# Other PSUM banks for the first projections of a hybrid decoder's mixer, and for what follows it

## The chip, the cores and the metric

The kernel runs on one core of one Trainium2 chip. The metric is the time of one execution on the device in microseconds, as the median of several runs. One execution was also taken by the hardware profiler; the views below come from it. The engines are TensorE (PE in the views; its weight loads, which overlap the matmuls, are PEld), VectorE (DVE), ScalarE (ACT), GpSimd (POOL) and SyncE (SP). TensorE writes to PSUM, 8 banks of 128 partitions by 512 fp32 values; VectorE and ScalarE read it from there.

## The reference

A decoder trunk of two layers, 512 tokens by 1024 channels, fp32. Each layer is

```python
x = x + 0.5 * swiglu(rms_norm(x, ffn1_norm[l]), ffn1_w_in[l], ffn1_w_out[l])
z = rms_norm(x, mix_norm[l]) @ mix_w_in[l]
z_fox, z_moba, z_rwkv = jnp.split(z, [FOX_IN, FOX_IN + MOBA_IN], axis=-1)
y = concatenate([fox_mixer(z_fox, ...), rwkv7_mixer(z_rwkv, ...), moba_mixer(z_moba, ...)])
x = x + y @ mix_w_out[l]
x = x + memory_cross_attention(rms_norm(x, xattn_norm[l]), rms_norm(mem, xattn_mem_norm[l]), ...)
x = x + 0.5 * swiglu(rms_norm(x, ffn2_norm[l]), ffn2_w_in[l], ffn2_w_out[l])
```

FoX is causal softmax attention with a forget gate (4 heads of 64), RWKV-7 a linear recurrence over the 512 tokens (8 heads of 64, done in blocks of 64 tokens, two heads at a time), MoBA a block-sparse causal attention (4 heads of 64). The cross-attention has 4 heads of 128 over 256 memory tokens.

## The kernel before

**Tiling.** x lies in SBUF transposed, 8 chunks of 128 channels by 512 tokens. All large matmuls are done in three passes: an operand is split into a high part (rounded to the matmul's fp32r) and a low rest, and `three` (lines 149 to 154) multiplies high by high, high by low and low by high into one PSUM bank. A projection of 128 columns (`zproj`) is 24 matmuls of 128x128 by 512 into one bank. Its weights are loaded by SyncE (`load_raw`, wraw, 3 buffers), and `split` (lines 137 to 147) makes whi on ScalarE and wlo on VectorE, two buffers each.

**Who empties a bank.** The norm's factor for each token is multiplied in when the bank is emptied on VectorE: `shift` (zt, line 523) for the projections of the recurrence, `heads_t` (p, line 499) for heads of the attentions. For this they need rsb, which comes from the norm's sum (`norm_sum`, line 247) and its spread over the partitions (`norm_spread`, line 256); the mixer issues the sum behind its first projection and the spread behind its second one.

**The mixer.** `ORDER` (line 37) is an order written out by hand: R, V and K with a number are the projections of the recurrence for one pair of heads, p stands for three more (p0 for decay and rate, p1 and p2 for the gates, p2 with the forget gates of FoX, 36 columns in all), fq, fk, fv, mq, mk, mv are the projections of the two attentions, s (scaled), g (gram), r (rows), i (inverse), t (transitions) and y (states) the six steps of the recurrence, and f with two digits a step of FoX's attention. A planner gives each engine its instructions in a fixed order before the run; it goes by priorities that fall along `ORDER`, with a lead for some kinds (`PRI`), and takes what it takes to be ready. So a unit that waits for a bank can be overtaken in the plan, but on the chip each engine's order is fixed.

**PSUM of the recurrence.** Eight banks in two pools, the first with ts twice and acc, the second with sp twice, tx, and ty twice: `RP` and `RPW`, lines 49 to 53. All first projections go to the one acc bank, but those that `ACC` (line 56) names: K0 to sp and p1 to tx. The ts banks belong to the transitions and the states, `TAGS`, and are first used by them after the first inverse. The scaled step, the norm's sum and spread and the forget gates use tx.

**PSUM of the mixer's end and the cross-attention.** `BP` and `BPW`: the first pool has acc twice and pt twice, the second po twice, the third sp twice. These pools lie over those of the recurrence, and a tile waits for the last reader of what lay in its bank. acc takes projections (of the memory and the queries) and the mixer's output projection, sp the scores, pt the transposed softmax, po the output of the attention and, under the name st, the norm's sum and spread. `ORDER2` has four kinds of work: steps of MoBA's attention (two digits), m (a piece of the memory's keys and values, `mem_kv`: transposes at line 1082, casts at 1086 and 1087, four key heads, two halves of the values), c (casts of the mixer's output) and w (its output projection). `ORDER3` is the cross-attention: sum, spread, z (a query projection), n (its norm), m, and attention steps.

Of the kernel before, what the change touches and what calls it, by code (L numbers as in the profile page):

```python
# [6 lines left out]
F32 = mybir.dt.float32  # L7
# [8 lines left out]
P = 128  # L16
# [24 lines left out]
ORDER2 = "31 11 10 m c0 01 21 00 c1 c2 m c4 x c5 c3 m c6 w3 m 20 m w6 m 30 w4 c7 w1 w5 w2 w0"  # L41

ORDER3 = "sum spread z1 z0 n1 z2 n0 m n2 02 z3 00 n3 12 03 10 13 01 11"
BP = {"acc": 2, "po": 2, "sp": 2, "pt": 2}

TAGS = {"s": "tx", "g": "ty", "r": "ty", "i": "ty", "t": "ts", "y": "ts"}

LATE = {"y2": 1, "G": 0, "Pf": 1, "KX": 1, "tk1": 0, "V2": 0, "gs0": 2, "gs1": 2, "ER": 1, "BN": 1, "KV": 2, "AR": 2, "tk2": 1, "g2": 1, "var": 2, "DC": 2, "p": 2, "a": 2, "zr": 0, "e": 0, "lw": 1, "zv": 1, "zk": 0}
RPW = {"ts": 0, "sp": 1, "acc": 0, "tx": 1, "ty": 1}
BPW = {"acc": 0, "sp": 2, "pt": 0, "po": 1}  # L50

RW = {"e": 2, "tk1": 2, "tk2": 2, "zr": 2, "zv": 2, "ER": 2, "zk": 2, "BN": 2}
RP = {"acc": 1, "tx": 1, "ty": 2, "ts": 2, "sp": 2}
WP = {"wraw": 3, "whi": 2, "wlo": 2}

ACC = {"K0": "sp", "p1": "tx"}
EARLY = 2

LINE = 512
# [39 lines left out]
def f32(ap):  # L99
    return ap.bitcast(F32)  # L100
# [15 lines left out]
class Trunk:  # L116
# [410 lines left out]
    def rwkv_prep(self, l, ap, rp, at, ab):  # L527
        nc, rw = self.nc, self.rw
        w = self.ins['mix_w_in'][l]
        self.tw = rw.tile([P, S], F32, name="tw", tag="tw")  # L530
        self.acc = ACC.get("p0", "acc")
        ps = self.zproj(ap, *self.weights(w[:, Z_LO:Z_LO + P]), P)
# [3 lines left out]
        for i, m in ((0, P), (1, 32)):  # L536
            g = rw.tile([P, S], F32, name=f"gs{i}", tag=f"gs{i}")
            self.acc = ACC.get(f"p{i + 1}", "acc")
            if i == 0:
# [469 lines left out]
    def softmax_pt(self, at, bp, sps, n):  # L1009

        nc = self.nc
        p = at.tile([P, 2, S], F32, name="p", tag="p")
        pT = at.tile([P, 2, S], F32, name="pT", tag="pT")
        mx = at.tile([P, 2], F32, name="mx", tag="mx")
        sm = at.tile([P, 2], F32, name="sm", tag="sm")
        for h in range(2):
            ph, m, s = p[:, h, :n], mx[:, h:h + 1], sm[:, h:h + 1]
            nc.vector.tensor_reduce(m, sps[h][:, :n], axis=AX.X, op=ALU.max, negate=True)
            nc.scalar.activation(ph, sps[h][:, :n], AF.Exp, bias=m, accum_out=s)
            nc.vector.reciprocal(s, s)  # L1020
            nc.vector.tensor_scalar(ph, ph, s, None, op0=ALU.mult)
            pt = bp.tile([P, 512], F32, name="pt", tag="pt" if "pt" in bp.bufs else "sp")
            for j in range(n // P):
                nc.tensor.transpose(pt[:, j * P:(j + 1) * P], ph[:, j * P:(j + 1) * P], self.ident)  # L1024
            self.cp(f"pT{h}", pT[:, h, :n], pt[:, :n])
        return pT.rearrange("p h (j q) -> p h j q", q=P)
# [86 lines left out]
    def xattn(self, l, xp, bp, mem):  # L1113
        nc = self.nc
        mm = nc.tensor.matmul
        oh = xp.tile([P, 4, S], F32R, name="oh", tag="oh")
        ol = xp.tile([P, 4, S], F32R, name="ol", tag="ol")
        w = self.ins['xattn_w_q'][l]
        fin = {}
        for o in self.order(ORDER3, PRI3, lambda o: "a" if o[0] in "01" else o[0]):  # L1120
            if o[0] == "z":
                h = int(o[1])
                q = xp.tile([P, S], F32, name=f"xqT{h}", tag=f"xqT{h}")
                fin[h] = q, self.heads_t(w[:, h * P:(h + 1) * P], bp, xp, bp, q, P, self.dpar[:, l, 13:14])
            elif o == "m":
                next(mem)
            elif o in ("sum", "spread"):
                getattr(self, "norm_" + o)(bp.tile([P, 512], F32, name="psx", tag="st"))
            elif o[0] == "n":
                fin[int(o[1])][1]()  # L1130
            else:
                u, t = int(o[0]), int(o[1])
                tq = slice(t * P, (t + 1) * P)
                sps = [bp.tile([P, 512], F32, name="sp", tag="sp") for _ in range(2)]
                for i in range(2):
                    mm(sps[i][:, :256], fin[2 * u + i][0][:, tq], self.mkT[:, 2 * u + i, :], start=True, stop=True)
                pT = self.softmax_pt(xp, bp, sps, 256)
                po = bp.tile([P, 512], F32, name="po", tag="po")
                for i in range(2):
                    h = 2 * u + i  # L1140
                    for j in range(2):
                        mm(po[:, i * P:(i + 1) * P], self.mv[:, j, h * P:(h + 1) * P], pT[:, i, j, :], start=j == 0, stop=j == 1)
                src = po[:, :256].rearrange("p (h q) -> p h q", h=2)
                o = oh[:, 2 * u:2 * u + 2, tq]
                nc.scalar.activation(o, src, AF.Copy)
                nc.vector.tensor_tensor(ol[:, 2 * u:2 * u + 2, tq], src, f32(o), op=ALU.subtract)
        return oh, ol

    def mixer_and_xattn(self, l):
        tc, nc = self.tc, self.nc  # L1150

        def sb(name, bufs=1):
            return tc.tile_pool(name=name, bufs=bufs, reuse_waits="tile")

        def pp(name, bufs=1):
            return tc.tile_pool(name=name, bufs=bufs, space=PSUM, reuse_waits="tile")
# [7 lines left out]
        with sb("raw") as raw:  # L1164
# [9 lines left out]
            with sb("rw") as rw0, sb("rwm") as rw1, sb("rwl") as rw2, pp("rp") as rp0, pp("rps") as rp1, pp("rpt") as rp2:  # L1174
# [55 lines left out]
                for o in self.order(ORDER, PRI, lambda o: "q" if o in parts and o != "p" else o[0]):  # L1230
                    self.acc = ACC.get(o, "acc")
                    if o in parts:
# [8 lines left out]
            with sb("kv") as kv, pp("bp") as bp0, pp("bps") as bp1, pp("bpt") as bp2:  # L1241
                bp = TagPool((bp0, bp1, bp2), BP, {"st": "po"}, BPW)
                mem = self.mem_kv(l, kv, bp)
# [120 lines left out]
```

## Time and profile before

| | us |
|---|---|
| median of 3 runs | 2577.13 (2576.03 to 2581.13) |
| profiled execution | 2587.6 |
| its span, first to last instruction | 2585.9 |
| TensorE busy | 2495.8 (97%) |
| VectorE, ScalarE, GpSimd busy | 1346.3, 864.3, 490.2 |
| mean granted clock of TensorE | 0.977 |

A line of a timeline reads: start, duration, engine, line, operation, output and inputs by the program's names, shape, count, and in brackets the idle time of the engine before it with what ended it. A line of the waits reads: who waited, for which instruction, total us, times, longest. In the table by stretches each engine has its busy time and its count; PEclk is the granted share of the full clock. Layer 0's mixer begins at 388, its recurrence ends at about 763, its cross-attention runs from 856 to 922; in layer 1 these are 1671, 2036, 2131 and 2195.

### The profile page before, as it was taken

The page shows a single profiled execution, that of the slowest core. Times are in us where ns is not written, and L with a number is a line of the kernel's source. Part 1 is how long each engine was busy: PE and PEld are TensorE (multiplying, and loading weights), DVE is VectorE, ACT ScalarE, POOL GpSimd, SP SyncE. Part 2 cuts the span into 40 slices and gives each one's busy share as a digit, 9 for nine tenths or more (in the row PEclk, how much of TensorE's full clock was granted, in tenths as well). Part 3 has the DMA queues.
Part 4 walks back from the last instruction along what each step waited for, and adds up shares of the span by engine and source line. Part 5 has one row for each costly group of instructions (what it writes and reads, how often), then busy time and mean ns, then how long its engine had stood idle before and what let it go on. Part 6 is the DMA issues. An engine that isn't in the chain of part 4 may idle for free.

```text
span 2585.9 us, 35209 instructions
## 1 busy us (share of the span) xinstructions
PE 2495.8 (97%) x13976; PEld 2030.0 (79%) x13976; DVE 1346.3 (52%) x2503; ACT 864.3 (33%) x1401; POOL 490.2 (19%) x613
## 2 busy tenths in 40 slices
PE   8999998999989899999999999998999899999999
PEld 6888886787768788888888888767877677888887
DVE  5434444666755664343444444455767666544444
ACT  4222232333343353232332222332334543422222
POOL 4212120222210122020221111202322110221211
PEclk9999999998979999999999999999989999999999
DMA  4333342221212223333333333422222121333332
GB/s 141 98 98 98 96 127 67 67 67 34 73 33 84 62 80 98 98 98 98 88 100 98 97 99 90 125 69 70 53 48 59 50 84 46 110 98 98 96 95 86
DMA packets 434880, 218.41 MB, mean 84 GB/s; under 512 B 63856, under 2 KB 428828, under 8 KB 434716
## 3 DMA queue, kind: packets, MB, share of 16 engines
q1 hardware_dynamic: 431948, 212.36, 29.0%
q10 hardware_dynamic: 2448, 2.76, 0.3%
q8 instruction: 110, 1.80, 0.3%
q0 software_dynamic: 320, 1.05, 0.1%
q14 instruction: 54, 0.44, 0.1%
HBM read 205.64 MB, written 10.49 MB: 84 GB/s over the span
## 4 chain that ended last, share of the span: by engine, by line
PE 86%; DVE 5%; POOL 2%; ACT 2%; DMA 2%; issue 1%; SPq 1%; ACTq 0%; POOLq 0%; DVEq 0%
PE acc L152 22%; PE acc L154 22%; PE acc L153 22%; PE po L1053 2%; PE sp L1041 1%; PE acc L950 1%; PE acc L951 1%; PE acc L952 1%; ACT whi L145 1%; POOL P L282 1%; PE pt L1024 1%; PE ty L720 1%; DVE wlo L146 1%; PE ts L860 1%; POOL T L282 1%
## 5 line engine op out<-in xcount | busy, mean ns | idle before, releaser
L145 ACT ACTIVATE whi<-wraw 128x1024 fp32r<-128x1024 f32 (+3 forms) x386 | 390.2, 1012 | 1142.5 <-PE acc L153 1051.3
L152 PE MATMUL acc<-xh,whi 128*128 128x512 f32 (+1 forms) x1776 | 701.3, 395 | 21.4 <-DVE p L499 7.3
L154 PE MATMUL acc<-xh,wlo 128*128 128x512 f32 (+1 forms) x1776 | 698.3, 393 | 1.3 <-DVE wlo L146 1.3
L153 PE MATMUL acc<-xl,whi 128*128 128x512 f32 (+1 forms) x1776 | 697.1, 393 | 0.0
L146 DVE TENSOR_TENSOR wlo<-wraw,whi 128x1024 fp32r<-128x1024 f32 (+3 forms) x386 | 541.9, 1405 | 97.2 <-ACT whi L145 88.4
L152 PEld LDWEIGHTS acc<-xh,whi 128*128 128x128 f32 (+1 forms) x1776 | 335.4, 189 | 98.4 <-ACT whi L145 9.1
L154 PEld LDWEIGHTS acc<-xh,wlo 128*128 128x128 f32 (+1 forms) x1776 | 335.5, 189 | 77.3 <-issue 3.0
L153 PEld LDWEIGHTS acc<-xl,whi 128*128 128x128 f32 (+1 forms) x1776 | 335.5, 189 | 70.1
L342 POOL TENSOR_TENSOR up<-up,g 128x512 f32<-128x512 f32 x88 | 118.6, 1348 | 998.6 <-ACT whi L145 900.5
L152 PE MATMUL acc<-th,whi 128*128 128x512 f32 x704 | 274.3, 390 | 1.0 <-ACT whi L145 1.0
L154 PE MATMUL acc<-th,wlo 128*128 128x512 f32 x704 | 274.9, 391 | 0.2
L153 PE MATMUL acc<-tl,whi 128*128 128x512 f32 x704 | 274.0, 389 | 0.0
L295 DVE SCALAR_TENSOR_TENSOR x<-acc,x 128x512 f32<-128x512 f32 x96 | 65.9, 690 | 277.0 <-PE acc L154 277.0
L341 DVE TENSOR_TENSOR up<-acc,rsb 128x512 f32<-128x512 f32 x88 | 60.8, 691 | 278.8 <-PE acc L154 278.8
L338 DVE TENSOR_TENSOR g<-acc,rsb 128x512 f32<-128x512 f32 x88 | 60.8, 691 | 191.2 <-PE acc L154 188.2
L154 PEld LDWEIGHTS acc<-th,wlo 128*128 128x128 f32 x704 | 132.1, 188 | 31.3 <-DVE wlo L146 4.2
L152 PEld LDWEIGHTS acc<-th,whi 128*128 128x128 f32 x704 | 132.2, 188 | 30.7 <-ACT whi L145 4.0
L153 PEld LDWEIGHTS acc<-tl,whi 128*128 128x128 f32 x704 | 132.2, 188 | 27.2
L240 POOL TENSOR_TENSOR sqacc<-sqacc,sq 128x512 f32<-128x512 f32 x48 | 75.3, 1569 | 378.7 <-ACT sq L239 242.9
L346 POOL TENSOR_TENSOR tl<-up,th 128x512 fp32r<-128x512 f32 x88 | 128.6, 1461 | 65.4 <-ACT th L345 65.4
L345 ACT ACTIVATE th<-up 128x512 fp32r<-128x512 f32 x88 | 55.7, 633 | 120.7 <-POOL up L342 120.7
L950 PE MATMUL acc<-whi,xh 128*128 128x256 f32 x256 | 76.7, 300 | 0.7 <-DVE zt L523 0.7
(354 smaller groups left out, 3119.8 us busy)
## 6 DMA issues: line engine op xcount, KB each, us to landing
wraw<-in_ffn_w_in_dram SPq DMA_DIRECT2D x176, 512.0 KB
wraw<-in_ffn_w_out_dram SPq DMA_DIRECT2D x64, 512.0 KB
wraw<-in_mix_w_in_dram SPq DMA_DIRECT2D x52, 512.0 KB
wraw<-in_ffn_w_out_dram SPq DMA_DIRECT2D x32, 384.0 KB
wraw<-in_xattn_w_kv_dram SPq DMA_DIRECT2D x16, 512.0 KB
wraw<-in_mix_w_out_dram SPq DMA_DIRECT2D x16, 384.0 KB
scx<-x SPq DMA_DIRECT2D x16, 256.0 KB
x<-scx SPq DMA_DIRECT2D x16, 256.0 KB
```

The costliest lines, as they stand in the source:

```text
L145: nc.scalar.activation(hv, v, AF.Copy)
L146: nc.vector.tensor_sub(lv, v, f32(hv))
L152: mm(ps, lh, rh, start=start, stop=False)
L153: mm(ps, lh, rl, start=False, stop=False)
L154: mm(ps, ll, rh, start=False, stop=stop)
L240: (nc.vector if m == KC - 1 else nc.gpsimd).tensor_tensor(self.sqacc, self.sqacc, sq, op=ALU.add)
L295: self.nc.vector.scalar_tensor_tensor(xm, ps, coef, xm, op0=ALU.mult, op1=ALU.add)
L338: nc.vector.tensor_tensor(g, pss[0], rsb, op=ALU.mult)
L341: nc.vector.tensor_tensor(up, pss[1], rsb, op=ALU.mult)
L342: nc.gpsimd.tensor_tensor(up, up, g, op=ALU.mult)
L346: nc.gpsimd.tensor_tensor(tl, up, f32(th), op=ALU.subtract)
L950: mm(o, a, wh[:, kk, :], start=k == 0, stop=False)
```

## The change

Three things. In the recurrence, V0, p2, K1 and V1 go to the two ts banks, by `ACC`. In the cross-attention, z2 goes to a po bank, by the same table, which `xattn` now reads. At the mixer's end, the two pt banks get names of their own, pt0 and pt1, one for each of the two heads of an attention step, and `BPW` lays the pools out anew: pt0 and po twice, then pt1 and acc twice, then sp twice.

```diff
-BP = {"acc": 2, "po": 2, "sp": 2, "pt": 2}
+BP = {"acc": 2, "po": 2, "sp": 2, "pt0": 1, "pt1": 1}
...
-BPW = {"acc": 0, "sp": 2, "pt": 0, "po": 1}
+
+BPW = {"pt0": 0, "po": 0, "pt1": 1, "acc": 1, "sp": 2}
...
-ACC = {"K0": "sp", "p1": "tx"}
+ACC = {"K0": "sp", "p1": "tx", "V0": "ts", "p2": "ts", "K1": "ts", "V1": "ts", "z2": "po"}
...
@@ softmax_pt
-            pt = bp.tile([P, 512], F32, name="pt", tag="pt" if "pt" in bp.bufs else "sp")
+            pt = bp.tile([P, 512], F32, name="pt", tag=f"pt{h}" if f"pt{h}" in bp.bufs else "sp")
...
@@ xattn
                 q = xp.tile([P, S], F32, name=f"xqT{h}", tag=f"xqT{h}")
+                self.acc = ACC.get(o, "acc")
                 fin[h] = q, self.heads_t(w[:, h * P:(h + 1) * P], bp, xp, bp, q, P, self.dpar[:, l, 13:14])
+                self.acc = "acc"
```

## Rows read from the trace of the kernel before

**Rows 1.** The page: TensorE's busy time, and the chain that ended last, by engine

```profile
PE 2495.8 (97%) x13976; PEld 2030.0 (79%) x13976; DVE 1346.3 (52%) x2503; ACT 864.3 (33%) x1401; POOL 490.2 (19%) x613
...
PE 86%; DVE 5%; POOL 2%; ACT 2%; DMA 2%; issue 1%; SPq 1%; ACTq 0%; POOLq 0%; DVEq 0%
```

**Rows 2.** The table by stretches, stages of layer 0, with its heading

```profile
core 0: us, PE busy (x) PEld busy (x) DVE busy (x) ACT busy (x) POOL busy (x), PEclk, DMA share, GB/s
390.00:441.00 51.00, 44.44 (x182) 32.96 (x182) 23.73 (x53) 15.73 (x21) 0.68 (x7) 0.93 0.26 65
...
690.00:763.00 73.00, 63.14 (x503) 44.92 (x502) 36.25 (x116) 28.94 (x72) 8.35 (x19) 0.75 0.08 19
763.00:856.00 93.00, 91.58 (x519) 73.14 (x518) 59.82 (x145) 40.42 (x90) 12.14 (x9) 0.98 0.30 93
856.00:922.00 66.00, 58.92 (x339) 48.19 (x338) 42.91 (x137) 26.21 (x66) 3.54 (x2) 0.97 0.15 45
```

**Rows 3.** TensorE's waits from 388 to 460, layer 0

```profile
PE acc L152 <- DVE zt L523: 2.3, 1, 2.3
PE acc L152 <- ACT whi L145: 1.9, 2, 0.9
PE acc L152 <- ACT e L641: 1.6, 1, 1.6
PE acc L154 <- DVE wlo L146: 0.7, 1, 0.7
PE acc L152 <- DVE p L499: 0.4, 1, 0.4
```

**Rows 4.** Timeline of TensorE, first projections of layer 0: V0, p0, p2

```profile
401.18 0.50 PE L152 MATMUL acc<-xh,whi 128*128 128x512 f32 x1 [2.34 <-DVE zt L523]
...
409.45 0.47 PE L152 MATMUL acc<-xh,whi 128*128 128x512 f32 x1 [0.93 <-ACT whi L145]
...
420.45 0.39 PE L152 MATMUL acc<-xh,whi 128*36 128x512 f32 x1
```

**Rows 5.** Timeline of VectorE: the evictions of R0, V0 and p2

```profile
400.44 0.68 DVE L523 TENSOR_TENSOR zt<-acc,rsb 128x512 f32<-128x512 f32 x1
...
408.61 0.69 DVE L523 TENSOR_TENSOR zt<-acc,rsb 128x512 f32<-128x512 f32 x1 [5.90 <-PE acc L154]
...
426.90 0.68 DVE L523 TENSOR_TENSOR zt<-acc,rsb 32x512 f32<-32x512 f32 x1
```

**Rows 6.** Timeline of ScalarE: the split of p2's weights

```profile
415.04 0.44 ACT L145 ACTIVATE whi<-wraw 128x288 fp32r<-128x288 f32 x1 [2.11 <-PE acc L153]
```

**Rows 7.** The table by stretches, around stretches of low clock and one in layer 1

```profile
402.00:405.40 3.40, 3.40 (x10) 2.63 (x9) 0.71 (x1) 0.00 (x0) 0.10 (x1) 0.50 0.49 144
...
757.00:767.20 10.20, 7.74 (x31) 5.99 (x32) 5.90 (x21) 6.01 (x14) 5.66 (x5) 0.50 0.20 61
...
873.00:876.40 3.40, 3.40 (x10) 2.65 (x9) 0.00 (x0) 0.57 (x1) 0.00 (x0) 0.50 0.23 67
...
1683.00:1690.00 7.00, 6.07 (x27) 4.70 (x27) 2.06 (x3) 2.20 (x3) 0.10 (x1) 1.00 0.29 75
```

**Rows 8.** Timeline of layer 0's cross-attention: z2 on TensorE, evictions on VectorE

```profile
872.36 0.50 PE L152 MATMUL acc<-xh,whi 128*128 128x512 f32 x1 [2.34 <-DVE p L499]
...
871.62 1.28 DVE L499 TENSOR_TENSOR p<-acc,rsb 128x512 f32<-128x512 f32 x2
```

**Rows 9.** Timeline of TensorE at the recurrence's end, layer 0

```profile
742.20 2.09 PE L1053 MATMUL po<-pT,fox 128*64 128x128 f32 x16
...
759.04 1.09 PE L930 MATMUL ts<-ident,tk 128*128 128x128 f32 x4 [3.35 <-DVE tk L923]
...
762.51 1.97 PE L1082 MATMUL acc<-ident,mtk 128*128 128x128 f32 x8 [0.40 <-DVE yr L934]
...
764.41 0.90 PE L1053 MATMUL po<-pT,mvv 128*64 128x128 f32 x3
```

**Rows 10.** One line's instructions: the memory's casts on VectorE, both layers

```profile
L1087 DVE SCALAR_TENSOR_TENSOR mhl<-acc,params,mhl x16: 467/474/484, 767.8 to 2047.6; 128x256 fp32r<-128x256 f32 x16
```

## Prediction

> **What bounds the kernel now.** I read the page's busy shares and its chain of work first: TensorE is busy 97% of the span and holds 86% of the chain that ended last [rows 1]. So an engine other than TensorE matters only where it makes TensorE wait, and the second view is the table by stage, in which the reader should compare the first figure after the length (TensorE's busy time) with the length itself. In layer 0 the mixer's first projections leave TensorE idle for 51.00 - 44.44 = 6.6 us, the recurrence's end for 73.00 - 63.14 = 9.9 us at a mean clock of 0.75, the mixer's end for 1.4 us only, and the cross-attention for 7.1 us [rows 2]. The halves of SwiGLU are full. The change touches just these four stages. Third, the list of TensorE's waits in the first 70 us of the mixer says by what it was held [rows 3], and the timelines around each wait say which resource that was.
>
> **First projections, gaps.** R0, V0, p0, p2, R1 and K1 share one bank before the change. TensorE starts V0 only at 401.18, after 2.34 us of nothing [rows 4], and VectorE's eviction of R0 ran from 400.44 for 0.68 us, to 401.12 [rows 5]. So that wait is for the bank. The next one is named after ScalarE's split, but the eviction of V0 ended at 408.61 + 0.69 = 409.30 and p0 started at 409.45 [rows 4, 5]; the one before R1 is named after e, and the eviction of p2 ended at 426.90 + 0.68 = 427.58, some 0.15 us ahead of R1's start [rows 5]. The view names the last event by its own clock; both fit the bank equally well, and the weights do not: the split of p2 (the only one of 288 elements) began at 415.04 [rows 6], while p2, the only group with 36 columns, began at 420.45 [rows 4], so a split runs one whole projection ahead. I therefore charge all of 2.3 + 1.9 + 1.6 to the bank, with the 0.4 before the projection after fk1, and also the 0.7 for wlo: K0 had overtaken the blocked V0 and met its own split unready [rows 3]. Sum: 6.9 us. With V0, p2, K1 and V1 in the two ts banks, no two neighbours of the order R0 V0 K0 p0 p1 p2 R1 K1 fk1 V1 use one bank, and an eviction (0.69 us) has the time of a whole projection to end in (24 matmuls; 27 kept TensorE busy for 6.07 us at full clock [rows 7], so about 5.4 us). Layer 1 shows the same five rows but for 0.5 in place of 0.7: 6.7 us. Both layers: **13.6 us**. The lower bound is 0 (the next wait ends as late, a rival below), the upper bound 13.6, since nothing shows more to take there. I take all of it, because these are stretches in which TensorE stood still with weights ready.
>
> What hangs on the moved steps: p2's bank is read by the gates and by the shift, both on VectorE; the gates and then s0 follow p2, so they come earlier with it. The new wait is that the transitions need the ts banks back from K1 and V1. Their evictions are over long before the first inverse is, so I cost it at nothing; if that cover were gone, one eviction (0.69 us) a layer would show in front of the transitions. No instruction and no DMA is added or dropped; loads of weights on SyncE's queue follow the splits and come earlier with them.
>
> [...]
>
> **Cross-attention.** z1, z0 and z2 share two acc banks, and z2 starts at 872.36, 2.34 us after the norm's spread, waiting for z1's eviction, which began at 871.62 behind a split on VectorE [rows 8]. In po, z2 needs only the bank of the norm's sum, which was read before the spread was even made. Two layers, the second by the same pattern, give **4.7 us**; 873.00 to 876.40 is a stretch at 0.50 in layer 0 [rows 7], another 1.7 us in one of the two. What is late next is the split for the memory projection that follows, about 1 us, which is late already. From 0 to 4.7 us, I take 4.7 for the same reason as above.
>
> **Banks at the mixer's end.** The banks of the mixer's end lie over the recurrence's. Before, the memory's transposes (L1082) start at 762.51, when VectorE has written yr from the last ts bank, so acc lies on ts; TensorE stood still for 3.35 us in front of L930 and 0.40 us in front of L1082 [rows 9]. The new layout puts po on the ts banks and acc further back, on banks that sp and tx held, which are free once the last FoX attention is out (its last value matmuls run from 742.20 for 2.09 us [rows 9]). So the memory's transposes, and after their casts the first key projections, can stand in those holes. po loses nothing: its first matmul starts at 764.41, after yr in any case [rows 9]. Upper bound: the idle of both layers, about 2 x 3.75 = 7.5 us, plus the clock of 757.00 to 767.20 (7.74 us of TensorE work at 0.50 [rows 7], up to 3.9 us a layer): 15. Lower bound: the memory's casts stand ahead of the last states on VectorE, 8 in a layer x 474 ns [rows 10] = 3.8 us, so -7.6 for both. I take **+3.5**, the side of the idle, because the transposes need 1.97 us [rows 9] and fit into the 3.35, and the planner may place only a part there.
>
> **Does it carry to the end?** Behind the recurrence TensorE is full (91.58 of 93.00 us [rows 2]), so what is saved up to there stays saved. Inside the recurrence the chain (s0, gram, inverse, transitions, states) begins after R1 and K1 and so moves with them.
>
> **Sum.** 13.6 + 4.7 + 3.5 = 21.8 us, and of the clock (2 x 1.7 in this execution) half, 1.7, since one layer in two paid: **23.5 us**. The profiled execution took 2587.6 us (its span 2585.9), 10.5 above the median of 2577.1; its low-clock stretches differ between the layers too, so I take the gain from the median: **2553.6 us**, 0.9% less. Against the profiled execution the same would be about 2564.
>
> **Rivals.**
> *Partial:* the planner leaves V0 behind the spread, or the ts banks are not free when wanted, and only the cross-attention and half of the first projections gain: 4.7 + 6.8 = 11.5, 2566 us. Speaks for it: the order is planned anew and can place anything in between. Against: no row shows V0 waiting for anything but the bank. 0.12.
> *Nothing gained:* the weights take the place of the bank. [...] As a mechanism here: if each split ended just when the eviction did, as the names in [rows 3] say, only V0's wait (2.34 us a layer) would go, 4.7 in all, and 2572 us would be left, just about no change. Against: the 288-element split ran 5.4 us ahead of its use [rows 4, 6]. 0.10 with all other ways of no change.
> *Slower:* projections fill TensorE while the recurrence's chain waits. If they run some 7 us ahead and the chain doesn't move with them, the fill is used up 7 us earlier, and 7 us more of the recurrence's end run with small matmuls alone, at the clock of 0.75 or lower that stage shows [rows 2]: the gain is given back, and up to 7 us a layer are added where the clock falls to half, 14 in all, less the 4.7 of the cross-attention: 2586 us. It decides from a lag of the chain of about 5 us a layer. For it: that stage's clock. Against: s0 depends on K0 and on p2's gates, which come earlier themselves. 0.10.
>
> **How the numbers follow.** Forecast 0.68, partial 0.12, none 0.10, slower 0.10. About 0.2% (5 us) is what a measurement of this kernel can tell from no change. Faster 0.80, same 0.10, slower 0.10. The range: all upper bounds, 13.6 + 4.7 + 15 + 3.4 = 36.7, give 2540; at the other end it takes in the partial case and no change, to 2578, and leaves out the slower rival.
>
> **What would show it.** Right: no wait in front of V0, p0, R1, K1 and z2 above 0.2 us; the stage of the first projections (to K1's end) 7 to 9 us shorter; L1082 ahead of L930, and the wait before L930 under 2 us. Wrong: K1's end 7 us earlier but L720's first gram matmuls where they were, with a longer last stretch of the recurrence; whi waits of about 1 us in the bank's place; casts of the memory between the last states.

## The result, and the profile of the changed kernel

The changed kernel takes 2555.64 us (median of 16 runs, 2544.29 to 2573.66) beside 2576.58 us for the kernel before in the same measurement: **0.9922 of its time, 95% interval 0.9898 to 0.9946**. A second measurement gave 0.9942 (0.9917 to 0.9968). The forecast was 2553.6, 0.991 of 2577.1. So the number was right; the experiments show that its terms were not all so. Medians of the kernel before differ from one measurement to the next (2570.86 to 2576.58), so only ratios are compared below. The spread within one kernel goes with TensorE's granted clock: of the 16 runs, 2573.66 us ran at a mean clock of 0.972 and 2546.57 us at 0.985.

The profiled execution took 2557.43 us. Its lines are one higher than before from L50 on (L152 is now L153), three higher in the cross-attention. Five stages of layer 0 in the table by stretches, answering to [rows 2]. They are cut at events (ffn1's norm sum, the end of K1's eviction, the first gram matmul, the ends of the third and fourth head's output, the sums of the cross-attention's and of ffn2's norm); after the length come busy time and count of PE, PEld, DVE, ACT and POOL, then TensorE's clock:

```profile
core 0: us, PE busy (x) PEld busy (x) DVE busy (x) ACT busy (x) POOL busy (x), PEclk, DMA share, GB/s
24.90:428.50 403.60, 401.60 (x1774) 327.81 (x1775) 184.47 (x245) 125.23 (x153) 73.89 (x63) 1.00 0.35 100
428.50:466.10 37.60, 30.79 (x129) 22.78 (x127) 22.23 (x62) 8.35 (x12) 4.93 (x7) 0.78 0.18 47
...
696.20:754.10 57.90, 53.45 (x484) 40.81 (x483) 30.99 (x98) 26.82 (x67) 1.89 (x2) 0.82 0.05 12
754.10:849.20 95.10, 91.47 (x487) 72.20 (x488) 59.54 (x140) 39.09 (x84) 16.22 (x12) 0.97 0.32 97
849.20:933.40 84.20, 80.10 (x432) 66.37 (x432) 56.76 (x158) 38.43 (x86) 8.68 (x6) 0.96 0.22 65
```

The first three of these stages in the kernel before, on the same cuts:

```profile
27.60:441.50 413.90, 406.87 (x1779) 331.47 (x1780) 184.79 (x246) 125.18 (x152) 73.89 (x63) 0.99 0.34 98
441.50:469.80 28.30, 26.12 (x125) 20.12 (x124) 20.29 (x57) 8.45 (x12) 4.71 (x7) 0.94 0.22 59
...
710.50:762.50 52.00, 45.38 (x324) 32.43 (x322) 24.17 (x82) 20.33 (x53) 1.48 (x2) 0.73 0.00 1
```

Up to K1's end TensorE stands still for 2.0 us, where the kernel before has 7.0 on the same cut. But the next stage, up to the first gram, has 6.8 us of idle time, 2.2 before, and a clock of 0.78, 0.94 before. TensorE's waits, 385 to 436 (answering to [rows 3]), then 428.5 to 466.2, and last the wait in front of the first gram in the kernel before:

```profile
PE acc L153 <- ACT rsb L259: 1.0, 1, 1.0
PE acc L155 <- DVE wlo L147: 0.4, 1, 0.4
PE acc L153 <- ACT whi L146: 0.3, 1, 0.3
...
PE ty L721 <- DVE B L283: 5.3, 1, 5.3
PE sp L603 <- DVE p L600: 1.5, 1, 1.5
...
PE ty L720 <- POOL B L282: 1.6, 1, 1.6
```

The waits for the bank are gone from the first list, and a wait of 5.3 us, 1.6 in the kernel before, stands in front of the first gram (L721); in layer 1 it is 6.72 us. How it comes about, in the timelines of TensorE and of VectorE:

```profile
435.11 0.48 PE L154 MATMUL acc<-xl,whi 128*128 128x512 f32 x1
...
441.79 0.39 PE L155 MATMUL acc<-xh,wlo 128*128 128x512 f32 x1
442.01 0.50 PE L645 MATMUL tx<-blk,e 128*128 128x2 f32 x4
...
445.68 0.63 PE L603 MATMUL sp<-ident,p 128*128 128x128 f32 x4 [1.55 <-DVE p L600]
...
451.35 0.79 PE L153 MATMUL acc<-xh,whi 128*128 128x512 f32 x1
...
458.85 0.60 PE L676 MATMUL tx<-ident,e 128*128 128x128 f32 x4
...
460.45 0.40 PE L155 MATMUL acc<-xh,wlo 128*128 128x512 f32 x1
466.14 2.08 PE L721 MATMUL ty<-ER,B 64*128 64x128 f32 x16 [5.29 <-DVE B L283]
```

```profile
453.89 0.43 DVE L673 COPY e<-rn 128x512 f32<-128x512 f32 x1
458.71 0.17 DVE L509 TENSOR_SCALAR hr<-sp 128x8 f32<-128x8 f32 x1 [4.39 <-PE sp L506]
...
471.64 0.69 DVE L500 TENSOR_TENSOR p<-acc,rsb 128x512 f32<-128x512 f32 x1
```

The projection from 435.11 to 442 is V1, now in a ts bank. It stands on TensorE's queue ahead of the first matmuls of the chain (L645); in the kernel before it ran from 455.66 to 461.44, behind those matmuls and just ahead of the transposes (462.09). From 451.35 on, 18 matmuls of fq1 stand ahead of the transposes of the norm (L676). Their input e was ready at 454.32; they ran at 458.85, and VectorE stood still for 4.39 us. Behind them VectorE and GpSimd need 7.3 us (458.85 to 466.14) to make the gram's operands, and for that time TensorE has only the last 6 matmuls of fq1, to 460.8. The next projection needs the acc bank, which fq1 holds until VectorE reads it at 471.64.

The recurrence's end, TensorE's timeline, answering to [rows 9], and two rows of the cross-attention, answering to [rows 8]:

```profile
735.09 1.05 PE L1083 MATMUL acc<-ident,mtk 128*128 128x128 f32 x8
...
744.48 0.39 PE L153 MATMUL acc<-mhl,whi 128*128 128x256 f32 x1
...
750.34 0.60 PE L931 MATMUL ts<-ident,tk 128*128 128x128 f32 x4
...
754.81 2.85 PE L1054 MATMUL po<-pT,mvv 128*64 128x128 f32 x16 [3.43 <-ACT yh L1279]
...
853.89 0.48 PE L153 MATMUL acc<-xh,whi 128*128 128x512 f32 x1
...
877.08 1.09 PE L514 MATMUL sp<-ident,hr 128*128 128x128 f32 x4 [2.79 <-DVE hr L270]
```

The memory's transposes (L1083) start 19 us ahead of y3's end (754.1), and 48 matmuls of its key projection (744.48 to 750.3) stand ahead of L931. The wait of 3.35 us in front of L931 is gone; one of 3.43 has come in front of po. z2 starts at 853.89 without a wait, and 2.79 us come later in front of L514.

### The profile page after: what moved, and what is told of

Read it like the earlier page. It is cut to its first block, busy times and chain, and to the rows that moved or that the text cites. A ratio compares the mean times of both kernels' runs of the same rounds, so it can differ in the third digit from the quotient of the medians.

```text
span 2555.7 us, 35229 instructions
## 1 busy us (share of the span) xinstructions
PE 2483.7 (97%) x13976; PEld 2018.3 (79%) x13976; DVE 1348.7 (53%) x2503; ACT 864.7 (34%) x1401; POOL 497.1 (19%) x613
## 4 chain that ended last, share of the span: by engine, by line
PE 87%; DVE 4%; POOL 2%; DMA 2%; ACT 2%; issue 1%; SPq 1%; POOLq 0%; DVEq 0%; ACTq 0%
PE acc L153 23%; PE acc L155 23%; PE acc L154 22%; PE po L1054 1%; PE sp L1042 1%; PE acc L951 1%; PE acc L953 1%; PE acc L952 1%; POOL P L283 1%; POOL T L283 1%; PE ts L861 1%; PE pt L1025 1%; PE ty L721 1%; DMA Tf<-scT 1%; PE sp L153 1%
## 5 line engine op out<-in xcount | busy, mean ns | idle before, releaser
L153 PE MATMUL acc<-xh,whi 128*128 128x512 f32 (+1 forms) x1776 | 698.0, 393 | 4.2 <-ACT whi L146 2.1
L153 PEld LDWEIGHTS acc<-xh,whi 128*128 128x128 f32 (+1 forms) x1776 | 334.3, 188 | 81.9 <-ACT whi L146 4.8
L153 PE MATMUL acc<-th,whi 128*128 128x512 f32 x704 | 274.2, 390 | 1.0 <-ACT whi L146 1.0
L153 PEld LDWEIGHTS acc<-th,whi 128*128 128x128 f32 x704 | 132.2, 188 | 30.7 <-ACT whi L146 4.0
```

The source lines that it names most:

```text
L153: mm(ps, lh, rh, start=start, stop=False)
```

## The experiments

All ratios are against the kernel before, run in the same measurement; figures in brackets are 95% intervals.

| run | what | ratio | interval |
|---|---|---|---|
| e1 | first projections alone | 1.0008 | 0.998 to 1.0035 |
| e2 | z2 alone | 0.999 | 0.9965 to 1.0015 |
| e3 | mixer's-end banks alone | 0.9962 | 0.9934 to 0.999 |
| e4 | all but z2 | 0.9952 | 0.9926 to 0.9978 |
| e5, e11 | all, but V1 in acc | 0.9931, 0.9901 | 0.9904 to 0.9958, 0.9865 to 0.9937 |
| e6 | all, and K2 in ts | 0.9946 | 0.9919 to 0.9973 |
| e7 | pt split alone | 1.0022 | 1.0001 to 1.0044 |
| e8 | new places alone, pt not split | 0.9982 | 0.996 to 1.0004 |
| e9 | first projections alone, V1 in acc | 0.9924 | 0.9896 to 0.9952 |
| e10 | all, once more | 0.9942 | 0.9917 to 0.9968 |
| e12 | all, V1 in sp | 0.9985 | 0.9965 to 1.0006 |

**The three parts alone (e1, e2, e3), and all but z2 (e4).** The first three are edits of the kernel before, e4 of the changed one.

```diff
e1  -ACC = {"K0": "sp", "p1": "tx"}
    +ACC = {"K0": "sp", "p1": "tx", "V0": "ts", "p2": "ts", "K1": "ts", "V1": "ts"}
e2  +ACC = {"K0": "sp", "p1": "tx", "z2": "po"}        (and the two lines in the cross-attention)
e3  +BP = {..., "pt0": 1, "pt1": 1}; BPW = {"pt0": 0, "po": 0, "pt1": 1, "acc": 1, "sp": 2}; tag=f"pt{h}"
e4  the changed kernel, less "z2": "po"
```

The two lines added in the cross-attention stand in e1, e3, and e7 to e9 below as well; they act only where `ACC` names z2.

> The first projections' banks alone (V0, p2, K1 and V1 in the ts banks); z2 and the banks at the mixer's end are as before. The sum on record has 13.6 us for this part, 15.3 with its clock: about 2561 beside 2576.6, and K1's end some 7 us earlier in each layer with the first gram matmuls as much earlier. Second theory, from the two traces: the projections run ahead, and the chain of the recurrence (s0, gram, inverse) does not move with them; TensorE then waits about 5 to 7 us in front of the first gram, and of 13.6 us only 0 to 6 are left: 2571 to 2577. Third (the slower rival): the fill that was used up early is missing at the recurrence's end, and the kernel is slower than before, 2580 to 2586.

> Only z2 is given another bank (po); all else as before. The sum on record: 4.7 us less, 2572. Second theory: the split of hr on VectorE ends nearly as late as the bank did, a new wait of some 2.8 us stands a projection later, and 1 to 2.3 us are left for both layers: 2574 to 2575.6, hardly to be told from no change.

> Only the banks at the mixer's end are laid out anew (acc behind po's place, pt split in two tags). The sum on record: 3.5 us less, bounds -7.6 to +15: 2573. Second theory, from the two traces: the memory's transposes and a whole key projection (some 5.4 us in a layer) move ahead of the last states, into time in which TensorE runs small matmuls with holes, so 5 to 7.5 us in each layer: 10 to 15 in all, 2562 to 2566.

> The whole change without z2's bank. The sum on record: 13.6 + 3.5 and the clock's 1.7, 2558; the full change should then be 4.7 us faster than this. Second theory: as the full change within 2 us, about 2557, and the parts add up (first projections 3 to 6, end banks 12 to 15).

e1 gains nothing: 1.0008, where the sum on record had 0.994. Its profile shows two places where the time goes back: the stage up to the first gram, and the stretch from the third to the fourth head's output. The table by stretches, layer 0 and then a stretch of each layer, and TensorE's timeline in front of the fourth inverse:

```profile
431.40:468.80 37.40, 30.58 (x129) 22.71 (x128) 22.23 (x62) 8.33 (x12) 4.99 (x7) 0.82 0.19 47
...
692.80:748.80 56.00, 49.47 (x418) 35.35 (x418) 26.20 (x87) 21.18 (x55) 1.38 (x2) 0.76 0.04 8
...
694.00:717.90 23.90, 23.80 (x228) 18.03 (x228) 6.27 (x16) 4.66 (x12) 0.00 (x0) 0.50 0.03 7
1970.60:1994.50 23.90, 22.19 (x219) 16.59 (x220) 6.26 (x18) 4.15 (x12) 0.00 (x0) 0.50 0.10 24
```

```profile
693.50 0.30 PE L813 MATMUL ty<-Tf,tk 64*64 64x64 f32 x2 [2.18 <-DMA Tf<-scT]
694.10 1.97 PE L813 MATMUL ty<-Tf,tk 64*64 64x64 f32 x30 [0.30 <-DMA Tf<-scT]
```

TensorE comes to the fourth inverse before its operand has come back from DRAM and waits 2.18 us in layer 0, and the clock is at 0.50 for the next 23.9 us; layer 1 has 23.9 us at 0.50 as well. e2's ratio of 0.999 can't be told from no change, nor from the 4.7 us (0.998) on record; its trace has the waits of the changed kernel, 2.8 us in front of L514 and none in front of z2. Of these three, e3 is the only part that is clearly faster by itself, about 9.8 us (2.6 to 17). Its table by stretches, y2 to y3 and y3 to the cross-attention's sum, both layers:

```profile
705.20:750.10 44.90, 40.06 (x379) 30.75 (x377) 28.90 (x91) 25.47 (x64) 1.85 (x2) 1.00 0.04 11
750.10:844.70 94.60, 90.45 (x487) 71.08 (x488) 59.84 (x140) 39.01 (x84) 16.24 (x12) 0.98 0.33 97
...
1966.00:2013.10 47.10, 42.29 (x380) 32.49 (x377) 28.62 (x92) 25.59 (x64) 1.30 (x1) 0.96 0.03 10
2013.10:2108.80 95.70, 91.60 (x487) 72.06 (x488) 60.01 (x141) 39.17 (x84) 16.28 (x12) 0.96 0.32 96
```

Work has gone from the second stretch into the first. The second is 8.0 and 8.3 us shorter than before. The first is 4.9 us longer in layer 1, where its clock is as before (0.96, 0.94); in layer 0 it is 7.1 us shorter, at a clock of 1.00 where the kernel before had 0.73. e4 lies between e3 and the changed kernel and is told apart from neither.

**V1 left out, and a fill for the new wait (e5, e6).** Edits of the changed kernel.

```diff
e5  -ACC = {..., "V0": "ts", "p2": "ts", "K1": "ts", "V1": "ts", "z2": "po"}
    +ACC = {..., "V0": "ts", "p2": "ts", "K1": "ts", "z2": "po"}
e6  +ACC = {..., "V0": "ts", "p2": "ts", "K1": "ts", "V1": "ts", "K2": "ts", "z2": "po"}
```

> The whole change, but V1 stays in the acc bank. Theory (the gain of the first projections is lost because one more whole projection, 24 matmuls, stands on TensorE's queue ahead of the chain gates, cumulative sum, norm of K, first gram): without V1's bank the planner has 1738 projection matmuls ahead of the transposes of the norm and 1762 ahead of the first gram, where the full change has 1780 and 1786. The first gram should then come 4 to 8 us earlier after ffn1's sum than in the full change (440.8 and 442.3 us there), the wait of 5.29 us in front of it fall below 2, and the kernel be 5 to 12 us faster than the full change: 2540 to 2550 beside 2576.6 of before. Rival: the chain's own length on VectorE and ScalarE sets the gram, it comes where it was within 2 us, TensorE waits longer in front of it, and the time is that of the full change or up to 5 us more.

> The whole change, with K2 in a ts bank too, so that one more projection can fill the wait of 5.29 us in front of the first gram, while fq1 still holds the acc bank (its result is read only at 471.6 us). If filling TensorE is what counts, the wait goes and the kernel gains 5 us a layer, 10 in all: 2546. If the chain is what counts, the first gram stays or comes later (1810 projection matmuls are ahead of it, 24 more than in the full change), the projection used early is missing at the recurrence's end, and the time is that of the full change within 4 us, or longer: 2552 to 2562.

In e5 the first gram comes 429.5 us after ffn1's norm sum in layer 0, 441.2 in the changed kernel, and its wait is 0.28 us: 12 us earlier, more than expected. The time, 0.9931, is not told apart from the full change's 0.9922, so of the expectation the half on the gram held and the half on the time was not shown. e6 puts one more projection under the gram's operands; idle time up to the gram falls from 6.8 to 4.1 us, the gram stays at 439.2, and the ratio, 0.9946, is that of the full change. Filling TensorE there is worth nothing that these runs can tell.

**The two halves of the mixer's-end banks (e7, e8).** Edits of the kernel before.

```diff
e7  +BP = {"acc": 2, "po": 2, "sp": 2, "pt0": 1, "pt1": 1}
    +BPW = {"acc": 0, "sp": 2, "pt0": 0, "pt1": 0, "po": 1}; tag=f"pt{h}"
e8   BP = {"acc": 2, "po": 2, "sp": 2, "pt": 2}
    +BPW = {"pt": 0, "po": 0, "acc": 1, "sp": 2}
```

> Of the banks at the mixer's end, only pt is split in two tags, one for each half of a pair; every bank lies where it was, and the rest is as before. If the place of acc and po carries the gain, this one is as before within 3 us, with the first memory transpose right behind y3 and the wait of some 3.4 us in front of the last states' transposes still there. If the split carries it, 8 to 10 us less than before.

> Of the banks at the mixer's end, only the places are changed (po and pt over ts and acc, acc over sp and tx), and pt stays one tag with two buffers; the rest is as before. If the places carry the gain: the memory's transposes start some 20 us ahead of y3's end, two projections (48 matmuls) stand ahead of the last states' transposes, and the time is 8 to 12 us under before. If the split was needed: within 3 us of before.

The split alone gains nothing (1.0022), and its first memory transpose stands right behind y3, after the same waits of 3.34 and 0.40 us. The places alone move the transposes 20 us ahead of y3's end, and the key projection with them, but 0.9982 is less than expected and not told from no change. So the places do what the trace of the changed kernel shows, and what that is worth lies between nothing and 10 us.

**First projections alone, without V1 (e9; kernel before with V0, p2 and K1 in ts), and the last three side by side (e10 to e12).**

```diff
e9  +ACC = {"K0": "sp", "p1": "tx", "V0": "ts", "p2": "ts", "K1": "ts"}
e10 the changed kernel;  e11 as e5
e12 as e5, and +"V1": "sp"
```

> The first projections' banks alone (as in the run that had them alone), but V1 stays in acc: V0, p2 and K1 in the ts banks, z2 and the mixer's end as before. Queue theory: the first projections gained nothing by themselves because V1's projection stood ahead of the chain; here the chain's norm and first gram stand one projection further ahead (1738 and 1762 projection matmuls before them, against 1780 and 1786), so the 5 us of idle time a layer saved up to K1 is kept: 8 to 10 us less than before. Fill theory: what is saved ahead of the gram is lost later in any case, since the recurrence's end then holds less work beside its chain: within 4 us of before. The first gram should come 12 us earlier by both.

> The changed kernel once more, beside the next two on one chip: 0.992 of before by its first timing, 0.990 to 0.995 expected. If the parts add up (first projections 1.001, z2 0.999, mixer's end 0.996, all but z2 0.995), 0.995 to 0.996.

> The whole change but V1 in acc, once more, beside the full change. Queue theory: 4 to 10 us faster than the full change, as the wait of over 5 us in front of the first gram is gone. Fill theory: the same time as the full change within 3 us.

> The whole change, with V1 in the sp banks. The chain's head stands as early as with V1 in acc (1738 and 1762 projection matmuls ahead), and V1 no longer waits for the eviction of the projection ahead of it; 27 fewer projection matmuls stand ahead of the first inverse. Queue theory: 2 to 6 us faster than V1 in acc. Fill theory: within 3 us of the full change, since idle time moves and does not go.

e9 answers the main question, whether V1's entry is what costs. The same edit as e1, less that entry, is at 0.9924 (19.6 us of 2572.8), and the two intervals don't overlap. Its rows for the same two stages, and TensorE's timeline in front of the first gram:

```profile
432.10:454.70 22.60, 21.99 (x105) 17.23 (x103) 16.83 (x52) 6.64 (x10) 4.86 (x6) 0.85 0.19 51
...
697.20:738.30 41.10, 33.76 (x309) 23.67 (x307) 23.74 (x81) 19.91 (x52) 1.35 (x2) 0.96 0.01 1
```

```profile
446.92 1.06 PE L676 MATMUL tx<-ident,e 128*128 128x128 f32 x4
447.66 0.79 PE L153 MATMUL acc<-xh,whi 128*128 128x512 f32 x1
...
453.44 0.39 PE L155 MATMUL acc<-xh,wlo 128*128 128x512 f32 x1
...
454.73 1.16 PE L721 MATMUL ty<-ER,B 64*128 64x128 f32 x16
```

Here one projection (fk1) stands between K1 and the transposes, and a whole one (V1, 24 matmuls, 447.66 to 453.8) covers the 7.8 us from the transposes to the gram. Counted on TensorE's queue, the projection matmuls from K1's last one to the transposes are 48 before, 66 in the changed kernel and 24 in e9; to the first gram 72, 72 and 48. The lengths of the stages in us, layer 0 and layer 1, cut as above:

| stage | before | e1 | e9 | e3 | changed | e11 |
|---|---|---|---|---|---|---|
| ffn1's sum to K1 | 413.9, 409.8 | 406.8, 404.5 | 406.6, 404.5 | 412.1, 409.8 | 403.6, 404.5 | 406.7, 404.5 |
| K1 to first gram | 28.3, 28.3 | 37.4, 36.0 | 22.6, 22.6 | 26.6, 28.3 | 37.6, 39.0 | 22.5, 24.5 |
| gram to y2 | 240.7, 243.7 | 224.0, 227.4 | 242.5, 247.2 | 239.8, 236.8 | 230.1, 223.4 | 243.7, 247.8 |
| y2 to y3 | 52.0, 42.2 | 56.0, 60.5 | 41.1, 42.2 | 44.9, 47.1 | 57.9, 53.3 | 48.6, 48.5 |
| y3 to xattn's sum | 102.6, 104.0 | 106.5, 105.4 | 104.0, 104.0 | 94.6, 95.7 | 95.1, 96.3 | 94.6, 94.9 |
| xattn to ffn2 | 85.6, 84.1 | 84.0, 85.6 | 84.0, 84.1 | 85.5, 83.9 | 84.2, 83.1 | 84.2, 83.3 |

The cut at y2 divides the work differently (from y2 to y3 the kernel before has 324 matmuls in layer 0, e1 418, e9 309), so those two stages are best read together. From the gram to y3 e9 needs 3.6 and 1.5 us more than e1 and does some 30 matmuls more: the earlier gram is kept to the end of the recurrence.

e11 is the fastest of all, 0.9901. On one chip it took 2549.39 us beside 2561.05 for the changed kernel (means 2550.9 of 6 and 2560.3 of 12 runs, a difference of 9.4 with a standard error of 3.5). Over both of their measurements the mean ratios are 0.9916 and 0.9932, 4 us apart. So leaving V1 in acc is likely the better kernel, by an amount between little and 12 us. e12 went against its expectation. The first gram is as early as in e11, but V1 now runs behind it (466.1 to 472.2), one projection fewer stands ahead of the first inverse, and TensorE waits for the inverses' operands. Its waits from the first gram to y2, layer 0, first line:

```profile
PE ty L813 <- DMA Tf<-scT: 8.0, 3, 4.8
```

In e9 the same line is 3.0 us. In e12, 2.8 us of it stand in front of the first inverse, where e9 has no wait, and 4.8 in front of the second. So my queue theory holds for the head of the chain and not as a rule that earlier is better: with 27 projection matmuls fewer in front of the first inverse its operand's way through DRAM is no longer covered, and 0.9985 is left.

**The clock of the runs.** Nearly every execution has its mean granted clock on record, and within one kernel the time falls by 2.1 us for each 0.001 of it (a straight line through 231 executions, with a level for each kernel in each measurement). With that slope the difference of the mean times can be split into what goes with the clock and what is left at equal clock. The split is an estimate, good to some 3 us; the kernel before comes out alike within 0.2 us in the three measurements that have its clocks.

| run | mean clock, before's | time less before's, us | with the clock | at equal clock |
|---|---|---|---|---|
| e1 | 0.9753, 0.9820 | +2.7 | +14.4 | -11.7 |
| e9 | 0.9832, 0.9819 | -17.3 | -2.8 | -14.5 |
| e2 | 0.9811, 0.9820 | -1.2 | +2.0 | -3.2 |
| e3 | 0.9839, 0.9820 | -10.5 | -4.0 | -6.4 |
| changed (e10) | 0.9774, 0.9819 | -13.8 | +9.6 | -23.4 |
| e11 | 0.9807, 0.9819 | -23.3 | +2.7 | -25.9 |
| e12 | 0.9769, 0.9819 | -3.4 | +10.7 | -14.0 |

So e1 does keep most of the waits that it ends, and gives the gain back through a lower clock; of the 20 us between e1 and e9, 17 go with the clock. TensorE's idle time in the profiled executions points the same way: 90.1 us before, 81.9 in e1, 74.7 in e9, 72.0 in the changed kernel. No run isolates what lowers the clock.

## Why the prediction was right in its number and not in all its terms

**First projections, gaps: 13.6 us. The gaps were right, what becomes of them was not.** Every wait charged to the bank is gone, and idle time up to K1 fell from 7.0 to 2.0 us in layer 0 and from 6.8 to 2.0 in layer 1, 9.8 in all (the waits that stay are rsb's and the splits', 1.7 us). The step that failed is the one under "Does it carry to the end?": that the chain begins after R1 and K1 and so moves with them. In the changed kernel, from ffn1's norm sum K1's end came 10.3 and 5.3 us earlier, the first gram 1.0 earlier and 5.4 later. (Some of that is the clock: K1 to the gram takes 37.6 us at 0.78, in e11 22.5 at 0.85, so that by 37.6 x 0.22 - 22.5 x 0.15, an estimate, about 5 of the 15 us are the clock's.) I treated the four bank moves as one edit. Three of them together (e9) end the waits and leave the chain's head early. V1's also lets a projection overtake the chain, because the order on TensorE is planned by what is free, and a free bank makes V1 free. With V1 left in acc the part measured 19.6 us (12 to 27), against 13.6 + 1.7 on record; with V1 moved, -2 us (-9 to +5). In time, the lower bound of 0 was the right value for the edit as it stood; at equal clock some 12 of the 13.6 us are there, and the lower clock takes them.

**What hangs on the moved steps.** "The new wait is that the transitions need the ts banks back" cost nothing, as said. The new wait that shows is the acc bank's, held by fq1 from 460.8 to 471.64 because VectorE was busy with the chain; I had not asked which engine reads a bank next. It is a sign and not the price: e6 puts the next projection in another bank and gains nothing.

**Clock: 1.7 us.** No run shows this term of the sum, a gain of 1.7 us by the clock; it was an estimate. What the runs showed in its place had the other sign: the changed kernel's executions ran at a mean clock of 0.9774 beside 0.9819, some 10 us lost. In the stage up to K1 the clock of layer 0 is 0.99 in the kernel before, e1, e3 and e9 and 1.00 in the changed one, with the holes and without. No run here shows that taking these idles away raises the clock of their own stage. What the clock cost stood elsewhere: 0.78 up to the gram in the changed kernel, with 436.00 to 439.40 and 446.20 to 456.50 at 0.50, and 23.9 us at 0.50 behind the fourth inverse's wait in e1. More banks gained nothing in e1 (1.0008), and e9's 0.9924 shows that more banks as such can gain here.

**Cross-attention: 4.7 us, right as far as it can be seen.** The waits of that stage listed by the view sum to 6.0 us before and 3.7 in the changed kernel, 2.3 less in a layer. z2's 2.34 are gone; 2.79 come in front of L514, and other waits of the stage shrink as much. Alone it measured 2.6 us, with an interval from -4 to +9 (3.2 at equal clock).

**Mixer's end: +3.5 us, too small, and for the wrong reason.** Alone it measured 9.8 (2.6 to 17), inside the bounds of -7.6 to +15. The order came as written: L1083 ahead of L931, no wait in front of L931. But idle time from y2 to the cross-attention is 9.0 and 8.9 us in e3 where it was 8.9 and 9.3: the wait went from L931 to po. "po loses nothing" left this wait out, though po itself is not late: it now starts 0.7 us behind y3's end (754.1), on banks that y3 held; the view names yh, so that it is the bank is read, not isolated. What fell is busy time (145.7 to 130.5 and 136.9 to 133.9 us), with the clock from y2 to y3 at 1.00 and 0.96 in place of 0.73 and 0.94. 48 matmuls of the key projection now stand among small ones there; that they raise the clock is not shown. Over the 12 executions of e3, 4 of some 10 us go with the clock and 6.4 are left at equal clock. How much of it is the places' stays open, since e8, with the same places, measured 0.9982 (1.7 us at equal clock).

**The sum, and the rivals.** 23.5 on record, 20.1 and 14.9 measured. Measured alone, one of the sum's parts gave nothing, one about what was written and one nearly three times as much. At equal clock the parts without the clock, 21.8 on record, are 23.4 in the changed kernel (e10), and the clock takes some 10 back where 1.7 were to be gained. So the size of the idle time was read well as a whole; that the total still came within 3.4 and 8.6 us of 23.5, with the clock's term wrong by some 11, is in part luck: with e1's clock 14 us would have gone instead of 10. Nothing-gained by the weights didn't happen (splits hold TensorE for 0.4 and 0.3 us up to K1), nor did the partial rival's reasons. The mechanism of the slower rival did, projections that run ahead while the chain doesn't move, with its sign at the gram (5.3 and 6.7 us) and at the recurrence's end (y2 to y3 4.0 and 18.3 us longer in e1, with some 100 matmuls more in it; from the gram to y3 e1 is 12.7 us shorter and 2.0 longer). It took back the whole of the first projections' gain, for the most part by the clock as that rival had it, and no more, so the kernel didn't become slower. "What would show it" had named this: K1's end 7 us earlier, the first gram where it was, a longer last stretch.

**What stays open.** By the ratios the parts don't add up: e9, e2 and e3 sum to 0.9876, and e5 and e11, which hold all three, have 0.9931 and 0.9901. At equal clock they do within the estimate: e1, e2 and e3 sum to 21.3 us beside 23.4 in the changed kernel, e9, e2 and e3 to 24.1 beside 25.9 in e11. What is open is the clock: what lowers it, and why V1's bank costs 8 in a thousand alone (e1 against e9) and between -1 and 4 beside the new mixer's end were not isolated; there y2 to y3 holds the key projection's 48 matmuls as well.

## What to carry to other kernels

A bank that ends a wait also changes the order of what a planner can start: give new banks one by one, and for each ask what its step will overtake. Where a serial chain on other engines follows, count the matmuls that stand ahead of each of its TensorE steps and those that cover its longest stretch off TensorE; time that is saved ahead of the chain is kept only if the chain's own steps move up too. And test a sum's terms singly, with the granted clock of every run beside its time: a right total was here one part that measured nothing and one that measured three times its term, and the part that measured nothing had gained some 12 us at equal clock.

## What the runs showed of the hardware

After a wait of 2.18 us in front of the fourth inverse the clock stayed at 0.50 for 23.9 us in layer 0 of e1, with TensorE busy for 23.80 of 23.90 us on 228 small matmuls; layer 1 had 23.9 us at 0.50 too, busy for 22.19 on 219. In e9 the fourth inverse stands ahead of y2, and y2 to y3, with 309 matmuls for e1's 418, took 41.1 us at 0.96 in place of 56.0 at 0.76. The kernel before shows the same in layer 0 alone, 27.3 us at 0.50 (702.40 to 729.70) that began within a wait of 2.37 us at the same place. I had priced a wait by its length; here the low clock cost more than the wait. The inverse's 30 matmuls (L813) took 1.97 us at 0.50 in e1, and in the kernel before 1.14 us at 1.00 (L812, from 503.10); by that ratio 23.80 us of work at 0.50 are some 10 us lost, an estimate.

The length of the low stretch goes neither with the place nor with the wait alone. At the same place in layer 1 the changed kernel had 6.8 us at 0.50 (1961.80 to 1968.60) that began within a wait of 2.66 us, a longer wait than e1's 2.18. The kernel before had waits of 0.38 and 0.44 us there and then 21.0 us at 1.00 (1989.00 to 2010.00). In layer 0 of the changed kernel 23.9 us at 0.50 (685.20 to 709.10) began some 10 us ahead of the wait of 1.17 us (from 694.84). What sets the length is not shown.
